# Hybrid decoder layer on one core: the last pair's candidate combination is emitted behind the gate matrices instead of ahead of them

## The chip, the cores and the metric

The kernel runs on one core of one Trainium2 chip. The metric is the device time of one execution in microseconds; the median of three runs of the kernel before is 3168.3 us (3166.18 to 3172.95).

## The reference, cut to what matters

One decoder layer over 1024 tokens of width 1024: a token mixer (dilated attention and a convolution module), a product-key expert layer (PEER), a gated embedding, a final norm. The change lies in PEER:

```python
s_half, i_half = lax.top_k(s, PEER_TOPK)            # 16 best of 128 keys, per token, head and half
cand = (s_half[:, :, 0, :, None] + s_half[:, :, 1, None, :])   # all pairs of the two halves
top_s, top_c = lax.top_k(cand, PEER_TOPK)           # 16 best pairs
expert = i1 * N_KEYS + i2                           # which of 16384 experts
gate = jax.nn.softmax(top_s, axis=-1)
h = einsum('td,tkd->tk', xb, expert_u[eb]);  act = gelu(h) * gb
y = einsum('tk,tkd->td', act, expert_v[eb])         # 128 experts per token (8 heads x 16)
```

## The kernel before, in words

The 1024 tokens are eight tiles of 128 (numbers 0 to 7), and they go through the mixer in four pairs. For every pair the program runs attention and convolution, the output projection, then the **search** (`search`, L467: matmuls with the keys, and on VectorE the 16 best keys per head and half) and the **combination** (`combine`, L499 to L576). The combination adds the 50 pairs of keys that can be among the best 16 (`cand`, L510), takes the 16 best (L520 to L524), a softmax over them (`gate`, L527 to L532, with an Exp on ScalarE at L528), and turns positions into two key numbers `i1` and `i2` by comparisons and sums over 128x2048 bf16 tiles (L535 to L575; two widening copies on ScalarE, L556 and L571).

Two kinds of tiles follow different routes:

- Tiles 2 to 5 (`ALL`) are the **dense tiles**. `gate_matrix` (L637 to L687) writes for each of their tokens the full 128 x 128 matrix of gates to HBM: per group of four tokens, two bf16 matmuls subtract the key number from the token's `i1` (`pd`, L659, L660, in one of three PSUM banks), VectorE turns that into `oa` (L668), `o2` is made on VectorE (L674) or, every second group, on ScalarE (L681, L682), four matmuls multiply them (`pG`, L685), ScalarE copies the result into `stage` (L686), and eight groups fill one stage of 2 MB that SP writes to `gate_d` (L687). That is 128 groups in all. `wide_input` (L689) prepares the tiles' input. Then `dense` (L704) goes through all 16384 experts in 32 steps on TensorE: `ph` (L741 to L743), `py` (L772 to L774).
- Tiles 0, 1, 6 and 7 (`FEW`) are the **gathered tiles**. `places` (L580) makes the expert numbers `ex` from `i1` and `i2` (L582). For each of 128 slots POOL fetches one row per token of `expert_u` and later of `expert_v` by an indirect DMA (L596), into six buffers, and VectorE consumes it: L609 (`u`, a dot product) and L625 (`v`, a sum into `gy`). That is 1024 fetches, tile by tile.

The four pairs are (0,1), (2,3), (4,5), (6,7). So the last pair's combination feeds only the gathered tiles 6 and 7, while the gate matrices need the combinations of the pairs (2,3) and (4,5).

The program is written with a tile framework: its scheduler sets each engine's own order of instructions at build time, by dependencies and by the order of emission, and each engine then works through its list in order. The gathers are written last (`gather_all`, L627), so they take the places on VectorE that other work leaves. What is emitted around the change:

```python
stage_search(NG - 1)                  # L885, search of tiles 6 and 7
stage_combine(NG - 1)                 # L886, their combination
for j, i in enumerate(ALL):           # L887
    gate_matrix(gp, j, *wide[i])      # L888, tiles 2 to 5
wide_input(h1, xh, xl)                # L889
gph.close()                           # L890, frees the space of the gate stages
```

Behind the dense steps, each tile goes through `embed` (L780): for the dense tiles 2 to 5 and the gathered tiles 0, 1, 6 and 7, the last of which is tile 7, whose input `gy` is the sum of its last fetches.

Of the kernel before, what the change touches and what calls it, by code (L numbers as in the profile page):

```python
# [26 lines left out]
NG = len(GROUPS)  # L27
# [74 lines left out]
def tile_layer(ctx, tc, t, consts, out):  # L102
# [38 lines left out]
    def rstd(srcs, n, name, junk=None, pool=small):  # L141

        ssq = pool.tile([P, len(srcs)], F32, tag="ssq", name=f"ssq_{name}", bufs=2)
        for j, src in enumerate(srcs):
            sq = junk(f"sqj_{name}_{j}") if junk else mpool.tile([P, D], BF16, tag="t2", name=f"sqj_{name}_{j}", bufs=3)
            S.activation(sq[:, :n], src, AF.Square, accum_out=ssq[:, j : j + 1])  # L146
        return inv_sqrt(ssq, 1.0 / n, name, pool)
# [432 lines left out]
    def places(i, i1, i2):  # L580
        ex = gpool.tile([P, SLOTS], I32, tag="ex", name=f"ex{i}", bufs=NF)
        V.scalar_tensor_tensor(ex, flat(i1), float(NK), flat(i2), ALU.mult, ALU.add)  # L582
        return ex
# [53 lines left out]
    def gate_matrix(gp, j, i1, i2, gate):  # L637

        tr = []
        for what, src in (("i2", i2), ("g", gate)):  # L640
            f = flat(src)
            if what != "g":
                f32 = mpool.tile([P, SLOTS], F32, tag="t2", name=f"gl{what}{j}", bufs=3)
                S.copy(f32, f)
                f = f32
            pt = pps(f"pgt{what}{j}")
            nc.tensor.transpose(pt[:, 0:P], f, ident)
            d = gp.tile([P, P], F32, tag=f"{what}T", name=f"{what}T{j}", bufs=2)
            S.copy(d, pt[:, 0:P])
            tr.append(d)  # L650
        i2T, gT = tr
        i2N = gp.tile([P, P], F32, tag="i2N", name=f"i2N{j}", bufs=2)
        S.activation(i2N, i2T, AF.Copy, scale=-1.0)
        four = [P, 4, NK]

        def less_keys(ix, t0, name):

            pd = lin(name).rearrange("p (t k) -> p t k", k=NK)
            nc.tensor.matmul(pd, flat(ix), ident16[:, t0 : t0 + 4].unsqueeze(2).to_broadcast(four), start=True, stop=False)  # L659
            nc.tensor.matmul(pd, ones16, minus16.to_broadcast([1, 4, NK]), start=False, stop=True)  # L660
            return pd

        for b in range(P // BT):
            stage = gp.tile([P, NK, BT], F32, tag="stage", name=f"stage{j}_{b}", bufs=2)
            for o in range(0, BT, 4):
                t0 = b * BT + o
                oa = gp.tile(four, F32, tag="oa", name=f"oa{j}_{t0}", bufs=2)
                V.scalar_tensor_tensor(  # L668
                    oa, less_keys(i1, t0, f"pd1_{j}_{t0}"), 0.0, gT[:, t0 : t0 + 4].unsqueeze(2).to_broadcast(four),
                    ALU.is_equal, ALU.mult,  # L670
                )
                o2 = gp.tile(four, F32, tag="o2", name=f"o2_{j}_{t0}", bufs=3)
                if o % 8 == 0:
                    V.tensor_tensor(  # L674
                        o2, i2T[:, t0 : t0 + 4].unsqueeze(2).to_broadcast(four),
                        iota.unsqueeze(1).to_broadcast(four), ALU.is_equal,
                    )
                else:

                    for e in range(4):  # L680
                        S.activation(o2[:, e, :], iota, AF.Abs, bias=i2N[:, t0 + e : t0 + e + 1])  # L681
                    S.activation(o2, o2, AF.Relu, bias=1.0, scale=-1.0)  # L682
                pg = sps(f"pG{j}_{t0}")
                for e in range(4):
                    nc.tensor.matmul(pg[:, rows(e)], o2[:, e, :], oa[:, e, :], start=True, stop=True)  # L685
                S.copy(stage[:, :, o : o + 4], pg.rearrange("p (t i) -> p i t", i=NK))  # L686
            nc.sync.dma_start(gd[j, :, :, b], stage.rearrange("p (q c) t -> p q (c t)", c=GROUP))  # L687

    def wide_input(h1, xh, xl):  # L689

        for q, h in enumerate(h1):
            r = rstd([h], D, f"wide{q}")
            xn = mpool.tile([P, D], F32, tag="xn", name=f"xw{q}", bufs=2)
            V.scalar_tensor_tensor(xn, h, r, g_ffn, ALU.mult, ALU.mult)
            for b in range(0, KD, 4):
                pt = pps(f"pt_xw{q}_{b}")
                for i in range(4):
                    nc.tensor.transpose(pt[:, rows(i)], xn[:, rows(b + i)], ident)
                hi, lo = (a[:, b : b + 4, rows(q)] for a in (xh, xl))
                pt = pt.rearrange("p (m c) -> p m c", c=P)  # L700
                S.copy(hi, pt)
                V.tensor_tensor(lo, pt, hi.bitcast(F32), ALU.subtract)
# [142 lines left out]
    def stage_search(g):  # L845
        st[g] = search(g, st[g])

    def stage_combine(g):
        vals, idxs = st[g]
        for j, i in enumerate(GROUPS[g]):  # L850
            if i in FEW:
                i1, i2, gate = combine(i, vals[j], idxs[j], gpool, NF)
                fetched[i] = (places(i, i1, i2), gate)
            else:
                wide[i] = combine(i, vals[j], idxs[j], mpool, ND)
# [27 lines left out]
    minus16 = gp.tile([1, 1, NK], BF16, name="minus16")  # L883
    V.tensor_scalar(minus16[:, 0, :], iota[0:1, :], -1.0, None, ALU.mult)
    stage_search(NG - 1)  # L885
    stage_combine(NG - 1)  # L886
    for j, i in enumerate(ALL):  # L887
        gate_matrix(gp, j, *wide[i])  # L888
    wide_input(h1, xh, xl)  # L889
    gph.close()  # L890
    den_in, du = scope(ctx, name="dupool", side="right")
# [90 lines left out]
```

## Time and profile before

| | us |
|---|---|
| median of three runs | 3168.3 |
| the profiled execution | 3160.1 |
| its span | 3158.3 |
| search of the last pair ends on VectorE | 1163.3 |
| first and last `pG` matmul of the gate matrices | 1192.1, 1408.7 |
| first dense matmul | 1437.9 |
| first matmul of the embeddings (L796) | 2963.1 |

| engine | busy, share of the span |
|---|---|
| TensorE (PE) | 87% |
| VectorE (DVE) | 79% |
| GpSimd (POOL) | 47% |
| ScalarE (ACT) | 36% |

Times of instructions are microseconds from the start of the span. A row of a timeline gives start, duration, engine, line, operation, what it writes and reads, and in square brackets the idle time of the engine before it with what ended that. The granted clock of TensorE is a share: 1.00 is 2.4 GHz, 0.50 is 1.2 GHz.

### The profile page before, as it was taken

The numbers are of one execution on the slowest core, as the hardware profiler recorded it, in microseconds if no ns is written. First come the engines' busy times: TensorE is split into PE (matmuls) and PEld (weight loads), VectorE is DVE, ScalarE is ACT, GpSimd is POOL, SyncE is SP. The second block draws the span as 40 slices with busy tenths as digits, with TensorE's granted clock in tenths as the row PEclk, the third lists the DMA queues.
The fourth block names the chain that finished last, engine by engine and source line by source line (L and its number), as shares of the span: only waits on it lengthen the run. The fifth ranks groups of instructions, "written<-read, shape, count | busy, mean of one in ns | idle before, by whom it ended". The sixth has DMA issues, their size and how long they took to land. (4 is left out here: it accounts for less than half of the span.)

```text
span 3158.3 us, 36012 instructions
## 1 busy us (share of the span) xinstructions
PE 2740.0 (87%) x11711; PEld 2003.6 (63%) x11711; DVE 2504.5 (79%) x5164; ACT 1132.6 (36%) x2082; POOL 1487.7 (47%) x1220
## 2 busy tenths in 40 slices
PE   6588959968995768987999999999999999999996
PEld 3465625853673455656777777777777777777643
DVE  1528777998898799886988888888988888988851
ACT  3523443264245228872232222232232232232342
POOL 0401675465445521224555556556655556555620
PEclk9798978988997888998999999999999999999998
DMA  5154859847953855999999999999999999999840
GB/s 164 54 179 148 311 200 347 293 147 260 338 188 129 321 202 169 284 274 345 340 333 343 322 339 344 356 340 351 332 323 344 353 329 349 348 324 335 323 159 23
DMA packets 304526, 865.75 MB, mean 274 GB/s; under 512 B 26778, under 2 KB 93746, under 8 KB 304338
## 3 DMA queue, kind: packets, MB, share of 16 engines
q0 software_dynamic: 147456, 536.94, 46.7%
q1 hardware_dynamic: 153616, 323.16, 29.7%
q10 hardware_dynamic: 3266, 3.36, 0.3%
q8 instruction: 92, 1.51, 0.2%
q14 instruction: 96, 0.79, 0.1%
HBM read 819.83 MB, written 43.52 MB: 273 GB/s over the span
## 5 line engine op out<-in xcount | busy, mean ns | idle before, releaser
L596 POOL DMA_INDIRECT u<-in_expert_u_dram,ex x512 | 654.4, 1278 | 830.1 <-DVE hk L609 568.0
L596 POOL DMA_INDIRECT v<-in_expert_v_dram,ex x512 | 682.3, 1333 | 513.0 <-DVE gy L625 380.6
L625 DVE SCALAR_TENSOR_TENSOR gy<-v,ga,gy 128x1024 f32<-128x1024 f32 x512 | 657.7, 1285 | 41.6 <-DMA v<-in_expert_v_dram,ex 32.6
L609 DVE CUSTOM_DVE_ANT_0 u<-u,gxn 128x1024 f32<-128x1024 f32 x512 | 613.1, 1226 | 52.3 <-DMA u<-in_expert_u_dram,ex 49.7
L741 PE MATMUL ph<-xh,uh 128*128 128x512 f32 x1024 | 407.1, 398 | 44.0 <-ACT uh L717 43.9
L743 PE MATMUL ph<-xh,ul 128*128 128x512 f32 x1024 | 409.4, 400 | 25.6 <-DVE ul L719 25.4
L742 PE MATMUL ph<-xl,uh 128*128 128x512 f32 x1024 | 405.1, 396 | 0.0
L759 ACT CAST vh<-v 128x1024 fp32r<-128x1024 f32 x128 | 131.5, 1051 | 749.0 <-PE kept_y L774 484.8
L741 PEld LDWEIGHTS ph<-xh,uh 128*128 128x128 f32 x1024 | 195.8, 191 | 91.8 <-ACT uh L717 51.9
L743 PEld LDWEIGHTS ph<-xh,ul 128*128 128x128 f32 x1024 | 195.6, 191 | 82.4 <-DVE ul L719 42.1
L350 POOL TENSOR_TENSOR side<-side,tap 128x256 f32<-128x256 f32 x192 | 150.8, 787 | 194.6 <-ACT tap L349 133.6
L761 DVE TENSOR_TENSOR vl<-v,vh 128x1024 fp32r<-128x1024 f32 x128 | 154.0, 1223 | 108.5 <-ACT vh L759 108.0
L772 PE MATMUL py<-vh,ah 128*128 128x512 f32 x512 | 204.0, 399 | 37.3 <-ACT ah L751 37.2
L270 PE MATMUL pq<-x2T,w_pq 128*128 128x256 f32 x1024 | 231.2, 384 | 5.6 <-DMA w_pq<-in_peer_wq_dram 3.9
L742 PEld LDWEIGHTS ph<-xl,uh 128*128 128x128 f32 x1024 | 195.9, 191 | 42.0
L270 PEld LDWEIGHTS pq<-x2T,w_pq 128*128 128x128 f32 x1024 | 194.6, 193 | 34.3 <-DMA w_pq<-in_peer_wq_dram 3.5
L773 PE MATMUL py<-vl,ah 128*128 128x512 f32 x512 | 200.4, 394 | 0.0
L774 PE MATMUL kept_y<-vh,al 128*128 128x512 f32 x512 | 199.7, 390 | 0.0
L772 PE MATMUL kept_y<-vh,ah 128*128 128x512 f32 x512 | 199.7, 390 | 0.0
L773 PE MATMUL kept_y<-vl,ah 128*128 128x512 f32 x512 | 199.5, 390 | 0.0
L774 PE MATMUL py<-vh,al 128*128 128x512 f32 x512 | 198.3, 395 | 0.3 <-DVE al L753 0.3
L717 ACT CAST uh<-u 128x1024 fp32r<-128x1024 f32 x128 | 134.1, 1048 | 113.7 <-DMA u<-in_uT_dram 80.2
(264 smaller groups left out, 4691.4 us busy)
## 6 DMA issues: line engine op xcount, KB each, us to landing
u<-in_uT_dram SPq DMA_DIRECT2D x128, 512.0 KB
v<-in_expert_v_dram SPq DMA_DIRECT2D x128, 512.0 KB
w_pq<-in_peer_wq_dram SPq DMA_DIRECT2D x64, 512.0 KB
gate_d<-stage SPq DMA_DIRECT2D x16, 2048.0 KB
gt<-gate_d SPq DMA_DIRECT2D x64, 512.0 KB
w_o<-in_w_out_dram SPq DMA_DIRECT2D x32, 512.0 KB
w_k<-in_w_qkv_dram SPq DMA_DIRECT2D x16, 512.0 KB
w_q<-in_w_qkv_dram SPq DMA_DIRECT2D x16, 512.0 KB
```

What stands on the lines that cost most here:

```text
L270: nc.tensor.matmul(a, w[:, k, :], xT[:, k, :], start=k == 0, stop=k == KD - 1)
L350: G.tensor_tensor(side, side, m, ALU.add)
L596: d = G.indirect_dma_start(out=e, out_offset=None, in_=table, in_offset=bass.IndirectOffsetOnAxis(ap=index, axis=0))
L609: uses(V.tensor_tensor_reduce(out=e, in0=e, in1=xn, scale=1.0, scalar=0.0, op0=ALU.mult, op1=ALU.add, accum_out=hk[:, k : k + 1]))
L625: uses(V.scalar_tensor_tensor(y, e, act[:, k : k + 1], y, ALU.mult, ALU.add))
L741: nc.tensor.matmul(ph, hi, xh[:, k, :], start=k == 0, stop=False)
L742: nc.tensor.matmul(ph, hi, xl[:, k, :], start=False, stop=False)
L743: nc.tensor.matmul(ph, lo, xh[:, k, :], start=False, stop=k == KD - 1)
L761: V.tensor_tensor(b, v, a.bitcast(F32), ALU.subtract)
L772: nc.tensor.matmul(py, ah[e][:, rows(j)], vh[e][:, half(f)], start=first, stop=False)
L773: nc.tensor.matmul(py, ah[e][:, rows(j)], vl[e][:, half(f)], start=False, stop=False)
L774: nc.tensor.matmul(py, al[e][:, rows(j)], vh[e][:, half(f)], start=False, stop=last_e)
```

## The change

The call that combines the pair (6,7) is emitted behind the four gate matrices.

```diff
@@ -883,9 +883,9 @@
     minus16 = gp.tile([1, 1, NK], BF16, name="minus16")
     V.tensor_scalar(minus16[:, 0, :], iota[0:1, :], -1.0, None, ALU.mult)
     stage_search(NG - 1)
-    stage_combine(NG - 1)
     for j, i in enumerate(ALL):
         gate_matrix(gp, j, *wide[i])
+    stage_combine(NG - 1)
     wide_input(h1, xh, xl)
     gph.close()
     den_in, du = scope(ctx, name="dupool", side="right")
```

Since the scheduler decides, three places of the engines' orders show what moves. On VectorE, behind the last operation of the search, first as it was before (`cand6` and `top6` are tile 6's candidates and its best ones, `oa0_0` and `o2_0_0` the first group of the first gate matrix):

```order
L496 MAX_INDEX idxs3_1_6393<-vals3_1_6392,sc3_3_1_6796 128x8 x2
L510 TENSOR_TENSOR cand6_6818<-vals3_0_6390 128x8x16
...
L535 CAST ix6_6875<-idxs3_0_6391 128x256
L520 MAX top6_6826<-cand6_6818 128x8 x2
...
L510 TENSOR_TENSOR cand7_6911<-vals3_1_6392 128x8x8
L668 SCALAR_TENSOR_TENSOR oa0_0_7017<-pd1_0_0_7018,gT0_7012 128x512
L530 TENSOR_REDUCE gs6_6871<-gate6_6868 128x8
L520 MAX top7_6919<-cand7_6911 128x8
```

and as it is with the change:

```order
L496 MAX_INDEX idxs3_1_6393<-vals3_1_6392,sc3_3_1_6796 128x8 x2
L668 SCALAR_TENSOR_TENSOR oa0_0_6831<-pd1_0_0_6832,gT0_6826 128x512
L674 TENSOR_TENSOR o2_0_0_6836<-i2T0_6822,cst_85 128x512
L668 SCALAR_TENSOR_TENSOR oa0_4_6844<-pd1_0_4_6845,gT0_6826 128x512
L674 TENSOR_TENSOR o2_0_8_6866<-i2T0_6822,cst_85 128x512
L510 TENSOR_TENSOR cand6_8818<-vals3_0_6390 128x8x16
...
L535 CAST ix6_8875<-idxs3_0_6391 128x256
L668 SCALAR_TENSOR_TENSOR oa0_8_6861<-pd1_0_8_6862,gT0_6826 128x512
L520 MAX top6_8826<-cand6_8818 128x8 x2
```

The first two `oa` and `o2` now stand ahead of the combination, and the rest of the combination is spread between the groups: `ex` of tile 6 (L582) stands behind 47 of the 128 `oa` (behind 1 before), that of tile 7 behind 85 (behind 12 before). Between the first and the last `oa` stood 40 `u` products of the gathers (L609); now 25 stand there, and 10 instead of 11 behind the last one, ahead of the dense steps. On SP a few transfers of the gathered tiles (L606, L926, L928) move by some places among the dense loads; POOL's order is unchanged.

On ScalarE, behind the squares of `wide_input`, before:

```order
L146 ACTIVATE sqj_wide3_0_9074,ssq_wide3_9073<-h1_5_4627 128x1024
L528 ACT_TABLE_LOAD
L528 ACTIVATE gate6_6868<-gate6_6868 128x128
L556 COPY ge6_6879<-p166_6877 128x2048
L571 COPY eq6_6900<-p166_6877 128x2048
L528 ACTIVATE gate7_6961<-gate7_6961 128x128
L556 COPY ge7_6972<-p167_6970 128x2048
L681 ACTIVATE o2_0_4_7035<-cst_85,i2N0_7014 128x128 x4
```

and with the change, there and, behind the dots, at the group of tokens 60 of the first matrix:

```order
L146 ACTIVATE sqj_wide3_0_9074,ssq_wide3_9073<-h1_5_4627 128x1024
L681 ACTIVATE o2_0_4_6849<-cst_85,i2N0_6828 128x128 x4
L682 ACTIVATE o2_0_4_6849<-o2_0_4_6849 128x512
...
L681 ACTIVATE o2_0_60_7061<-cst_85,i2N0_6828 128x128
L528 ACT_TABLE_LOAD
L528 ACTIVATE gate6_8868<-gate6_8868 128x128
L686 COPY stage0_1_6952<-pG0_56_7050 128x128x4
```

The Exp of tile 6 and that of tile 7 each stand between groups now, each with a table load ahead of it and, behind it, one for the next square root (L151): four loads among the gate matrices, where there were two, one of them ahead of the first group.

On VectorE, in the embeddings behind the dense steps, before (`v7_125` to `v7_127` are tile 7's last fetched rows, `sg1_4` the gate of the embedding of tile 4):

```order
L813 TENSOR_TENSOR sg1_4_18621<-sg1_4_18621,plp4_1_18623 128x512
L625 SCALAR_TENSOR_TENSOR gy7_21633<-v7_125_22010,ga7_21630,gy7_21633 128x1024
L814 TENSOR_TENSOR h1_4_4625<-h1_4_4625,sg1_4_18621 128x512
L625 SCALAR_TENSOR_TENSOR gy7_21633<-v7_126_22013,ga7_21630,gy7_21633 128x1024
L625 SCALAR_TENSOR_TENSOR gy7_21633<-v7_127_22016,ga7_21630,gy7_21633 128x1024
L153 RECIPROCAL r_fin4_18633<-sd_fin4_18631 128x1
```

and with the change, there and at the end of the gathers:

```order
L813 TENSOR_TENSOR sg1_4_18621<-sg1_4_18621,plp4_1_18623 128x512
L625 SCALAR_TENSOR_TENSOR gy7_21633<-v7_108_21959,ga7_21630,gy7_21633 128x1024
L814 TENSOR_TENSOR h1_4_4625<-h1_4_4625,sg1_4_18621 128x512
...
L813 TENSOR_TENSOR sg0_0_19501<-sg0_0_19501,plp0_0_19503 128x512
...
L625 SCALAR_TENSOR_TENSOR gy7_21633<-v7_127_22016,ga7_21630,gy7_21633 128x1024
L813 TENSOR_TENSOR sg1_0_19517<-sg1_0_19517,plp0_1_19519 128x512
```

At the same operation of tile 4 the gathers are 17 rows behind; the last one stands directly ahead of the second half of tile 0's embedding (`sg1_0`). Behind the last addition of the dense steps (L778) there are 56 `v` sums, where there were 40; in the dense steps themselves the number is the same, 20 or 21 a step. On TensorE the order behind the dense steps is unchanged.

## Rows read from the trace of the kernel before

**Rows 1.** Busy time of each engine by stretch; then clock, DMA share, GB/s.
```profile
core 0: us, PE busy (x) PEld busy (x) DVE busy (x) ACT busy (x) POOL busy (x), PEclk, DMA share, GB/s
1163.30:1192.00 28.70, 1.12 (x2) 0.10 (x1) 28.70 (x179) 8.16 (x10) 0.00 (x0) 0.50 0.00 1
...
1199.10:1409.00 209.90, 204.24 (x1282) 139.28 (x1280) 184.60 (x303) 183.36 (x454) 40.45 (x41) 1.00 0.83 252
1163.30:1409.00 245.70, 212.10 (x1309) 144.79 (x1308) 219.29 (x490) 197.08 (x476) 40.45 (x41) 0.92 0.71 216
1500.00:2900.00 1400.00, 1325.93 (x5672) 1067.92 (x5671) 1228.85 (x1609) 370.18 (x478) 825.30 (x602) 0.99 0.94 339
2963.00:3060.00 97.00, 96.89 (x279) 48.24 (x280) 68.88 (x69) 37.44 (x81) 44.38 (x37) 0.97 0.68 248
```

**Rows 2.** Timeline of TensorE: start, duration, instruction, idle time before it.
```profile
1172.86 0.58 PE L659 MATMUL pd<-ident,i 128*128 128x512 bf16 x1 [13.17 <-DVE oa L668]
...
1192.11 2.07 PE L685 MATMUL pG<-oa,o 128*128 128x128 f32 x8 [18.13 <-DVE o L674]
...
1195.39 3.78 PE L685 MATMUL pG<-oa,o 128*128 128x128 f32 x16 [0.24 <-ACT o L682]
...
1407.80 1.16 PE L685 MATMUL pG<-oa,o 128*128 128x128 f32 x8 [1.35 <-ACT o L682]
```

**Rows 3.** Timeline of VectorE, from the end of the search to `ex` of tile 7.
```profile
1163.31 0.96 DVE L510 TENSOR_TENSOR cand<-vals 128x128 f32<-128x128 f32 x7
...
1172.13 0.68 DVE L668 SCALAR_TENSOR_TENSOR oa<-pd,gT 128x512 f32<-128x512 f32 x1
...
1191.37 0.68 DVE L674 TENSOR_TENSOR o<-i2T,cst 128x512 f32<-128x512 f32 x1
...
1215.26 0.28 DVE L582 SCALAR_TENSOR_TENSOR ex<-i,i 128x128 int32<-128x128 bf16 x1
```

**Rows 4.** VectorE's groups from 1163.2 to 1217: busy, mean ns, idle before.
```profile
L668 DVE SCALAR_TENSOR_TENSOR oa<-pd,gT 128x512 f32<-128x512 f32 x13 | 8.8, 681 | 1.8 <-PE pG L685 1.8
L674 DVE TENSOR_TENSOR o<-i2T,cst 128x512 f32<-128x512 f32 x7 | 4.8, 684 | 0.0
```

**Rows 5.** VectorE's group of `u` products from 1300 to 1400.
```profile
L609 DVE CUSTOM_DVE_ANT_0 u<-u,gxn 128x1024 f32<-128x1024 f32 x19 | 23.0, 1216 | 0.0
```

**Rows 6.** Timeline of ScalarE: last square, a widening copy, a table load between two groups.
```profile
1164.80 0.19 ACT L146 ACTIVATION_READ_ACCUMULATOR sqj_wide<-h 128x1 f32 x1
...
1182.59 1.90 ACT L571 COPY eq<-p 128x2048 bf16<-128x2048 bf16 x1 [9.49 <-DVE p L569]
...
1211.56 0.58 ACT L686 COPY stage<-pG 128x512 f32<-128x512 f32 x1
1212.16 1.28 ACT L151 ACT_TABLE_LOAD   x1
1213.45 0.30 ACT L151 ACTIVATE sd_wide<-ssq_wide,eps 128x1 f32<-128x1 f32 x1
```

**Rows 7.** Waits of SP's queue from 1380 to 1450: total, times, longest.
```profile
SPq L715 <- DMA gate_d<-stage: 22.5, 1, 22.5
```

**Rows 8.** Timeline of VectorE behind the dense steps.
```profile
2948.68 1.28 DVE L625 SCALAR_TENSOR_TENSOR gy<-v,ga,gy 128x1024 f32<-128x1024 f32 x1 [1.47 <-DMA v<-in_expert_v_dram,ex]
...
2965.36 1.28 DVE L625 SCALAR_TENSOR_TENSOR gy<-v,ga,gy 128x1024 f32<-128x1024 f32 x1 [1.27 <-DMA v<-in_expert_v_dram,ex]
...
3030.23 2.60 DVE L625 SCALAR_TENSOR_TENSOR gy<-v,ga,gy 128x1024 f32<-128x1024 f32 x2
...
3059.96 0.69 DVE L813 TENSOR_TENSOR sg<-sg,plp 128x512 f32<-128x512 f32 x1 [7.17 <-PE plp L812]
...
3126.46 0.16 DVE L153 RECIPROCAL r_ple<-sd_ple 128x1 f32<-128x1 f32 x1 [1.00 <-ACT sd_ple L151]
```

**Rows 9.** Timeline of POOL: two fetches of tile 7, first and last of 33.
```profile
2973.73 1.01 POOL L596 DMA_INDIRECT v<-in_expert_v_dram,ex  x1 [0.30 <-issue]
...
3024.72 1.01 POOL L596 DMA_INDIRECT v<-in_expert_v_dram,ex  x1 [0.30 <-issue]
```

## The prediction

> **What bounds the kernel now.** I read the stretches first. In the dense steps TensorE is busy 1325.9 of 1400 us at a granted clock of 0.99, with VectorE at 1228.9 [rows 1]: TensorE sets the pace, and VectorE has little room beside it. The 97 us behind them are full too, 96.9 us of TensorE [rows 1]. So whatever lets the dense steps start earlier moves all that follows, unless something else holds the end. The stretch to look at is the one just ahead, the gate matrices. There, from 1163.3 to 1192.0, TensorE is busy 1.1 of 28.7 us and its clock is at 0.50, the lower of its two levels, while VectorE is busy all of the time [rows 1]. The timeline of TensorE names the wait: 13.17 us for `oa`, then 18.13 us for `o2`, both VectorE's, until the first `pG` at 1192.11 [rows 2]. And the timeline of VectorE says what it did instead: the candidates of tile 6 from 1163.31, the first `oa` only at 1172.13, the first `o2` at 1191.37, the last operation of the combination at 1215.26 [rows 3]. From 1199.1 to 1409.0 the picture is the other one: TensorE is busy 204.2 of 209.9 us at full clock, VectorE 184.6, ScalarE 183.4 [rows 1]. That part is TensorE's.
>
> **The price of the combination.** From 1163.31 to the end of `ex` at 1215.54 are 52.2 us. Of these VectorE was idle 1.8, and 13 `oa` took 8.8 and 7 `o2` took 4.8 us [rows 3, 4]. The remainder, 52.2 - 15.4 = 36.8 us, is the combination of two tiles, with a few small things. No gate matrix reads it. The edit removes none of it; it lets the groups of gate matrices go ahead, and the order of VectorE confirms that: two `oa` and two `o2` now stand directly behind the search.
>
> **The start, a gain.** The search ends at 1163.31, where the combination starts today. One `oa` and one `o2` behind it (0.68 us each [rows 3, 4]), so at 1164.7, the first `pG` can start, and not at 1192.11: 27.4 us earlier. ScalarE is ready for the second group soon after: its last square ends at 1164.99 [rows 6], and the Exp that stood next is gone from there. Beyond that, the first groups today run at the lower clock: 8 `pG` rows take 2.07 us there, 16 take 3.78 [rows 2], and a `pd` takes 0.58. TensorE would wait from 1159.7 to 1164.7, 5 us, and not until 1192.1 [rows 2]. If it keeps its clock it saves, over the first three groups and their `pd`, about half of the time from 1192.1 to 1199.1, up to 3 us; if not, nothing. I take 1.6, in the middle. Together 29 us.
>
> **What it costs in the gate matrices.** The combination is now work between the groups, and each engine works in order. Does it fit? VectorE was busy 219.3 us from 1163.3 to 1409, with everything in it; between the first and the last `oa` now stand 25 products of the gathers where 40 stood, and 15 x 1.22 = 18.3 us go [rows 1, 5]. That leaves 201 us. ScalarE has 197.1 us there and gets two more table loads of 1.28 us: about 200 [rows 1, 6]. TensorE needs the 209.9 us from the third group on. So TensorE remains the longest, but the other two are at 95%, and there are only three banks of `pd` to take up unevenness. The lower bound of the new stalls is 0, since by the sums all fits; the upper is the whole 36.8 us, if every operation of the combination stood in TensorE's way. I take 6, near the lower end, because the totals leave 9 us of room and the order spreads the combination over 85 groups: the two table loads (2.6 us) and of each of the four widening copies of 1.90 us [rows 6], which stand between copies out of PSUM, nearly half.
>
> On such a load the row shows 1.28 us, from 1212.16, with the copy ahead of it ended at 1212.14 and the next activation at 1213.45 [rows 6]: nothing around it. The Trainium skill speaks more strongly against the change here (ScalarE: Activation LUTs, section What ACT_TABLE_LOAD costs): about 1283 ns for the load plus about 1380 ns of drain, 2.66 us for a switch to another set. By that the two loads would be 5.3 us and my sum some 3 us worse; the trace has the load but not the drain, and the trace decides.
>
> **From the gate matrices to the dense steps.** The first dense load waits 22.5 us for the last stage to be written [rows 7], because it takes that space. Nothing of this changes: 10 products of the gathers stand there, where 11 stood. It moves with the stages. On SP and POOL only the place of a few loads of the gathered tiles among the dense loads shifts by some rows; if one came too late, it would cost one fetch, under 3 us. The combination issues no DMA.
>
> **The dense steps** keep 20 or 21 gathered rows a step in both orders, so they keep their pace and move as a block: 0.
>
> **The end, a small loss.** Sixteen products that no longer fit among the gate matrices push the gathers back: 56 sums, not 40, stand behind the dense steps. The last two now start at 3030.23 and end at 3032.8 [rows 8]. At POOL's rate there, 33 fetches in 50.99 us from first to last [rows 9], 1.59 us each, sixteen more end 25.5 us later relative to the dense steps, at what is 3058.3 in today's count. The next operation behind them on VectorE is `sg` of tile 0, ready at 3059.96 because TensorE delivers then [rows 8]. That is just in time, with other work in between, so I put 2 us, between 0 and 6. Tile 7's own embedding needs `gy` only before 3126.46 [rows 8] and has ample room. The three embeddings at the end are serial and move as they are.
>
> **Sum.** -29 + 6 + 2 = **-21 us**. On the profiled execution, 3160.1 us (its span of 3158.3 and 1.8 around it), that is 3139.1. The median of the three runs stands 8.2 us above that execution; I take this distance along: 3168.3 - 21 = **3147.3 us**, faster by 0.7%.
>
> **Rivals.**
>
> *The gathers hold the end.* If the sixteen deferred fetches cost what they cost just behind the dense steps, where VectorE waited for their DMA, seven in 16.7 us from 2948.68 to 2965.36, so 2.8 us from one to the next [rows 8], they need 45 us where 27.2 are free (3059.96 less 3032.8). Then tile 0's embedding and the three behind it come 18 us late: -29 + 6 + 18 = -5, 3163 us. For it: VectorE works in order, and the embeddings stand behind the fetches. Against it: those waits fell where the embeddings' weights were loaded, and from 2973.73 POOL kept to 1.59. Chance 0.10, half of it within 0.2%.
>
> *VectorE becomes the bound of the gate matrices, and the kernel is slower.* Place: the 85 groups between which the combination lies. Mechanism: TensorE has three banks ahead; whenever a long bf16 operation or one that waits for ScalarE stands ahead of an `oa`, TensorE runs dry. If all 36.8 us come out as waits, the sum is -29 + 37 + 2 = +10: 3178 us. It turns the sign once TensorE loses over 27 us, three quarters of the combination. For it: two engines at 95% in a fixed order. Against it: VectorE's sum is 201 against 210, and its products of the gathers, already in such places, left TensorE busy 204.2 of 209.9 us [rows 1]. Chance 0.06.
>
> *Between the two*, half of the combination shows as waits: -29 + 18 + 3 = -8, 3160 us. Chance 0.08, three quarters faster.
>
> *The change doesn't do what it says*, because the scheduler decides. The orders exclude most of that; what is left is that the combination's spread hides something that I don't see, with no change in time, 3168 us. Chance 0.03.
>
> **How the numbers follow.** The forecast has 0.73; its own range, with stalls of 1 to 13 us, the clock's 0 to 3 and the end's 0 to 6, is 3139 (-31 + 1 + 0, rounded) to 3160 (-27 + 13 + 6). To hold 8 in 10 the range takes in the rival of the end: 3139 to 3163. A measurement of this kernel can tell about 0.2%, 6.3 us, from no change. Faster by more: 0.73 + 0.05 + 0.06 = 0.84. Within it: 0.05 + 0.02 + 0.03 = 0.10. Slower: 0.06.
>
> **What would show it.** The first `pG` starts within 2 us of the end of the search, and the granted clock stays near 1.00 there. The last `pG` comes 20 to 26 us earlier, and the same shift stands at the first dense matmul and at the first of the embeddings. Between the groups VectorE is nearly full, with little of TensorE idle. The last `v` sum ends at about the same absolute time as now, some 25 us later relative to the dense steps. I would be wrong if TensorE showed repeated waits for `oa` between the groups, adding up to more than 15 us, or if TensorE waited behind the embeddings of tiles 5 and 0.

## The result, and the profile after

The changed kernel takes 3133.5 us (median of 4 runs, 3130.95 to 3141.12); the kernel before, timed beside it, takes 3167.5 us. The ratio is 0.9904, with a 95% interval of 0.9877 to 0.9931. It is faster, as forecast, but by more: 3133.5 lies 13.8 us below the forecast of 3147.3 and below the range, which began at 3139. The profiled execution of after took 3130.95 us with a span of 3129.1, 29.2 us less than the span before.

TensorE's timeline shows where they come from. A row gives start, duration, instruction, and in brackets the idle time before it.

```profile
1162.76 0.33 PE L647 MATMUL pgti<-cst,gli 128*128 128x128 f32 x1 [0.36 <-ACT gT L649]
1167.95 0.58 PE L659 MATMUL pd<-ident,i 128*128 128x512 bf16 x1 [4.86 <-DVE oa L668]
1168.55 4.20 PE L685 MATMUL pG<-oa,o 128*128 128x128 f32 x24
1172.68 0.39 PE L660 MATMUL pd<-minus,ones 1*128 1x512 bf16 x1
```

The waits of 13.17 and 18.13 us of before [rows 2] are now one of 4.86, and three groups of `pG` (24 rows) are through at 1172.75. On VectorE the first `oa` follows the last row of the search at once, and the combination (L510 and on) begins behind the second `o`:

```profile
1167.03 0.28 DVE L496 FIND_INDEX8 idxs<-vals,sc 128x8 uint32<-128x128 f32 x1
1167.23 0.67 DVE L668 SCALAR_TENSOR_TENSOR oa<-pd,gT 128x512 f32<-128x512 f32 x1
1167.82 0.68 DVE L674 TENSOR_TENSOR o<-i2T,cst 128x512 f32<-128x512 f32 x1
1168.41 0.68 DVE L668 SCALAR_TENSOR_TENSOR oa<-pd,gT 128x512 f32<-128x512 f32 x1
1169.02 0.68 DVE L674 TENSOR_TENSOR o<-i2T,cst 128x512 f32<-128x512 f32 x1
1169.62 0.97 DVE L510 TENSOR_TENSOR cand<-vals 128x128 f32<-128x128 f32 x7
```

The same stretches as in [rows 1], busy time of PE, PEld, VectorE, ScalarE and POOL, then the granted clock:

```profile
1167.20:1172.75 5.55, 4.79 (x26) 4.08 (x25) 5.55 (x24) 5.04 (x14) 0.00 (x0) 0.64 0.00 0
1172.75:1383.20 210.45, 203.07 (x1284) 140.27 (x1284) 193.71 (x436) 192.58 (x463) 23.99 (x25) 1.00 0.72 211
1167.20:1383.20 216.00, 207.85 (x1309) 144.36 (x1308) 199.26 (x458) 197.63 (x476) 23.99 (x25) 0.99 0.70 206
1500.00:2900.00 1400.00, 1332.31 (x5694) 1075.77 (x5693) 1228.64 (x1609) 372.36 (x478) 829.31 (x604) 0.99 0.93 339
2930.00:3030.00 100.00, 95.66 (x279) 47.52 (x280) 90.68 (x87) 38.02 (x82) 64.08 (x55) 0.98 0.93 339
```

The whole combination now lies between the groups, and behind the third group VectorE is busy 193.71 of 210.45 us where it was 184.60 of 209.90; TensorE's time for these groups is the same within 0.7 us. The dense steps look as before. Behind them the deferred sums fill VectorE: 90.68 of 100 us against 68.88 of 97.

TensorE's waits from 1150 to 1440 (total, times, longest):

```profile
PE ph L741 <- DMA gt<-gate_d: 29.0, 1, 29.0
PE pd L659 <- DVE oa L668: 6.3, 5, 4.9
PE pG L685 <- ACT o L682: 3.9, 7, 1.2
PE pG L685 <- DVE oa L668: 1.0, 1, 1.0
PE pG L685 <- ACT stage L686: 0.8, 1, 0.8
```

All waits for `oa` but the first come to 2.4 us. The 29 us ahead of the first dense matmul stand as they did; the row for SP's wait is this one, where before had 22.5 [rows 7]:

```profile
SPq L715 <- DMA gate_d<-stage: 22.7, 1, 22.7
```

To set executions side by side I take six marks, as the first and last starts of a line's instructions give them; for after (ns min/median/max, then first and last start):

```profile
L496 DVE FIND_INDEX8 idxs<-vals,sc x128: 274/284/292, 218.1 to 1167.0; 128x8 uint32<-128x128 f32 x128
L685 PE MATMUL pG<-oa,o x1024: 272/275/583, 1168.5 to 1382.9; 128*128 128x128 f32 x171
L741 PE MATMUL ph<-xh,uh x1024: 387/389/793, 1412.2 to 2903.4; 128*128 128x512 f32 x171
L796 PE MATMUL pt_ple<-dg,h x112: 273/276/583, 2927.8 to 3072.6; 128*128 128x128 f32 x112
L625 DVE SCALAR_TENSOR_TENSOR gy<-v,ga,gy x512: 1244/1284/1767, 661.9 to 3028.0; 128x1024 f32<-128x1024 f32 x171
```

The table holds the same marks of all profiled executions, in us. "Search" is the start of its last row (L496); first `pG`, last `pG` and first `ph` count from there; "dense" runs from the first `ph` to the first matmul of an embedding (L796); the last `v` sum (L625) and the end of the span count from that one. In before, that matmul starts at 2957.4; the 2963.1 of the table ahead of the prediction is its second group of rows, behind a wait of 4.63 us.

| kernel | search | first `pG` | last `pG` | first `ph` | dense | last `v` | end | span |
|---|---|---|---|---|---|---|---|---|
| before | 1163.1 | +29.0 | +245.6 | +274.8 | 1519.5 | +74.1 | +200.9 | 3158.3 |
| before_again | 1161.4 | +29.0 | +248.8 | +277.8 | 1518.6 | +74.3 | +201.2 | 3159.0 |
| after | 1167.0 | +1.5 | +215.9 | +245.2 | 1515.6 | +100.2 | +201.3 | 3129.1 |
| after_again | 1175.8 | +1.5 | +217.5 | +246.9 | 1521.4 | +100.3 | +201.4 | 3145.5 |
| no_combine | 1172.4 | +1.5 | +216.1 | +247.2 | 1518.5 | +66.7 | +201.9 | 3140.0 |
| twice | 1168.6 | +1.5 | +220.5 | +245.7 | 1509.9 | +147.8 | +208.5 | 3132.7 |
| four_times | 1166.0 | +1.6 | +219.0 | +293.4 | 1517.4 | +165.5 | +208.2 | 3185.0 |
| half | 1153.9 | +9.5 | +229.5 | +260.6 | 1523.5 | +92.8 | +201.6 | 3139.6 |
| behind_wide | 1162.6 | +1.5 | +216.0 | +246.8 | 1517.0 | +106.4 | +201.2 | 3127.6 |
| one_gate_first | 1228.0 | -143.9 | +164.4 | +194.6 | 1514.5 | +106.9 | +203.3 | 3140.4 |
| gates_first | 1393.8 | -303.2 | -88.2 | +53.6 | 1522.5 | +74.2 | +203.1 | 3173.0 |

From before to after: the search ends 3.9 us later and the dense steps are 3.9 us shorter, neither of which the change touches; last `pG` -29.7; from there to the first `ph` +0.1 (0.0 unrounded); end +0.4. Together -29.2.

### The profile page after: what moved, and what is told of

It reads as the page before. It is cut to its first block, busy times and chain, and to the rows that moved or that the text cites. A ratio compares the mean times of both kernels' runs of the same rounds, so it can differ in the third digit from the quotient of the medians.

```text
span 3129.1 us, 36005 instructions
## 1 busy us (share of the span) xinstructions
PE 2734.5 (87%) x11711; PEld 2003.1 (64%) x11711; DVE 2503.7 (80%) x5164; ACT 1133.9 (36%) x2084; POOL 1495.5 (48%) x1220
## 5 line engine op out<-in xcount | busy, mean ns | idle before, releaser
L596 POOL DMA_INDIRECT u<-in_expert_u_dram,ex x512 | 675.9, 1320 | 822.3 <-DVE hk L609 547.1
L596 POOL DMA_INDIRECT v<-in_expert_v_dram,ex x512 | 671.5, 1312 | 510.7 <-DVE gy L625 376.9
L625 DVE SCALAR_TENSOR_TENSOR gy<-v,ga,gy 128x1024 f32<-128x1024 f32 x512 | 657.8, 1285 | 41.0 <-DMA v<-in_expert_v_dram,ex 31.9
L609 DVE CUSTOM_DVE_ANT_0 u<-u,gxn 128x1024 f32<-128x1024 f32 x512 | 613.7, 1226 | 54.5 <-DMA u<-in_expert_u_dram,ex 53.4
L350 POOL TENSOR_TENSOR side<-side,tap 128x256 f32<-128x256 f32 x192 | 147.8, 772 | 193.8 <-ACT tap L349 132.4
```

What stands on the lines that cost most here:

```text
L350: G.tensor_tensor(side, side, m, ALU.add)
L596: d = G.indirect_dma_start(out=e, out_offset=None, in_=table, in_offset=bass.IndirectOffsetOnAxis(ap=index, axis=0))
L609: uses(V.tensor_tensor_reduce(out=e, in0=e, in1=xn, scale=1.0, scalar=0.0, op0=ALU.mult, op1=ALU.add, accum_out=hk[:, k : k + 1]))
L625: uses(V.scalar_tensor_tensor(y, e, act[:, k : k + 1], y, ALU.mult, ALU.add))
```

## The experiments

**The two kernels again**, unchanged, to see how far two executions of one kernel lie apart (no edit).

> The kernel before, unchanged, once more, to see how far its stages move from one execution to the next. Theory A (the gain is the wait of TensorE ahead of the gate matrices, 27.4 us, and some 3 us of slow clock behind it; what the profile shows besides is spread): the time is that of before within 0.2%; the end of the search moves by some 4 us between executions (1163.3 here, 1167.2 in the changed kernel), and so does the length of the dense steps, from the first ph at 1437.9 to the first matmul of the embeddings at 2957.4, 1519.5 us, against 1515.5 in the changed kernel. Theory B (the change also shortened the dense steps): the dense steps take 1519.5 us within 1 us again.

> The changed kernel, once more, timed in five rounds. Theory A: 29 to 31 us faster than before (ratio 0.990 to 0.991), gate matrices from the end of the search to the last pG 215 to 217 us. Theory B: 33 to 35 us faster (0.989), with dense steps of 1515.5 us within 1 us again, 4 less than before. My prediction's sum (21 us, ratio 0.9934) would need 6 us of stalls in the gate matrices, so 222 us there.

The kernel before came to 3163.7 us, ratio 1.0005 (0.9982 to 1.0028) to its other runs; the change to 3144.2 us, 0.9928 (0.9899 to 0.9956). The change's second trace has the same first `pG`, 1.5 us behind the search, and the same gate matrices within 1.6 us. Its search ends 8.8 us later than in the first trace and its dense steps take 1521.4 us. So the idea that the change shortens the dense steps (1515.6 against 1519.5) has no support: these two stretches vary by that much with nothing changed. The gate matrices of before vary too, 216.6 us in the first trace and 219.8 in the second, where TensorE's mean granted clock over them is 0.98 and 0.97. Differences of 3 us between two single traces of this stretch mean little, therefore, unless the clocks are alike.

**no_combine** leaves the last pair's combination out; tiles 6 and 7 fetch by the numbers and gates of tiles 0 and 1.

```
-    stage_combine(NG - 1)
+    fetched[6], fetched[7] = fetched[0], fetched[1]
```

> The combination of the pair (6,7) is left out altogether; tiles 6 and 7 fetch with the expert numbers and gates of tiles 0 and 1. Left out: 36.8 us of VectorE, 8 us of ScalarE, two table loads. Theory A (all of the combination lies hidden in the changed kernel): the same time as the changed kernel within 2 us, and the gate matrices take 209 to 211 us from the third group on, as with the combination (211.3). The prediction's theory (some 6 us of it stand in TensorE's way): 5 to 7 us faster than the changed kernel.

3139.0 us, ratio 0.9924 (0.9900 to 0.9948). Without the combination the gate matrices take 214.6 us from first to last `pG`; with the change they take 214.4 and 216.0. Taking the combination out altogether wins nothing more that the times show. The comparison is not clean, though. First no_combine, then after, from the first `pG` to the end of the last:

```profile
1173.93:1388.81 214.88, 210.38 (x1308) 145.55 (x1308) 184.64 (x299) 185.67 (x463) 43.55 (x45) 0.98 0.84 254
1168.55:1383.20 214.65, 207.27 (x1308) 144.35 (x1308) 197.91 (x455) 196.31 (x473) 23.99 (x25) 0.99 0.71 207
```

VectorE is only 13 us less busy, not 36.8, because products of the gathers move into the free places (56.89 us of them, 31.87 with the change). And TensorE's clock was lower by a hundredth, which is worth about 2 us of 215 (an estimate from the two rows). So a price of 2 or 3 us for the combination is not excluded; the 5 to 7 us expected from the prediction's theory did not show.

**twice** computes the combination a second time behind the gate matrices; what it gives is not read.

```
     stage_combine(NG - 1)
+    for j in range(2):
+        combine(16 + j, st[NG - 1][0][j], st[NG - 1][1][j], mpool, ND)
```

> The combination of the pair (6,7) is computed a second time behind the first, and nobody reads the second result. 36.8 us more of VectorE, 8 of ScalarE and two more table loads in the gate matrices, and 21 fewer products of the gathers there (4 where 25 stood), so VectorE has about 200 + 37 - 26 = 211 us and ScalarE 208 beside TensorE's 210: no room is left. Theory A (nothing shows as long as the sums fit): the gate matrices grow only by a few us, 3 to 10, and 22 more v sums stand behind the dense steps (79 for 57), which at 1.5 us each is 33 us more than the changed kernel has, where its own last sum is just in time; so the end is held by the gathers, 25 to 35 us later there, and the time is about that of before, 3160 to 3175. If VectorE's stalls set in well before the sums are full, the gate matrices grow by 20 us and more as well, and the time is 3185 or more.

3141.8 us, ratio 0.9933 (0.9913 to 0.9953): the time of the change. The gate matrices grew by a few us, as expected, but the time of 3160 to 3175, with the end held by the gathers, missed. VectorE's stretch shows why the work still fits:

```profile
1168.60:1389.00 220.40, 208.91 (x1292) 145.53 (x1292) 206.63 (x598) 203.56 (x480) 3.75 (x4) 0.98 0.54 153
```

Twice the combination, yet VectorE is only at 206.63 us, since 4 products of the gathers are left among the gate matrices where the change has 25: the order pushes them out behind, 21 of 1.22 us, 25.6 us. The gate matrices are 3 to 5 us longer, not 37, and 1.1 of it stands in the first three groups, which took 5.29 us at the lower clock where the change's trace has 4.20. In the order, 79 `v` sums now stand behind the dense steps (57 with the change, counted in the same way), the last one 47.6 us later than with the change, and the end moves by 7 us only.

**half** puts tile 6's part of the combination ahead of the gate matrices again and leaves tile 7's behind.

```
-    def stage_combine(g):
+    def stage_combine(g, only=(0, 1)):
...
+            if j not in only:
+                continue
...
     stage_search(NG - 1)
+    stage_combine(NG - 1, (0,))
     for j, i in enumerate(ALL):
         gate_matrix(gp, j, *wide[i])
-    stage_combine(NG - 1)
+    stage_combine(NG - 1, (1,))
```

> Of the last pair's combination, tile 6's part stands ahead of the gate matrices again, tile 7's stays behind them; 29 products of the gathers lie among the gate matrices (25 with the whole change, 40 before). Theory A (the gain is the wait for the combination, which TensorE no longer spends idle): half of the wait comes back. The first pG starts 13 to 17 us behind the search, where it was 29 before and 1.5 with the change, the clock falls to its lower level in that wait, and the time is 13 to 19 us above the change's. Theory C (the gain comes from the products of the gathers that left the stretch, which relieved VectorE): 11 of the 15 are gone, so nearly all of the gain stays; at most 8 us above the change's.

3149.1 us, ratio 0.9945 (0.9924 to 0.9966), 16.0 us above behind_wide, which ran on the same chip. The first `pG` comes 9.5 us behind the search, sooner than the 13 to 17 expected, because the first `oa` is taken in among tile 6's operations:

```profile
1162.75 0.59 PE L659 MATMUL pd<-ident,i 128*128 128x512 bf16 x1 [12.36 <-DVE oa L668]
1163.35 2.08 PE L685 MATMUL pG<-oa,o 128*128 128x128 f32 x8
...
1168.06 3.58 PE L685 MATMUL pG<-oa,o 128*128 128x128 f32 x16
```

```profile
1153.90:1171.64 17.74, 8.23 (x30) 5.84 (x29) 17.74 (x101) 9.81 (x19) 0.00 (x0) 0.50 0.00 1
```

But the clock is then at its lower level, 0.50, and stays there over the first three groups, which end at 1171.64, 17.7 us behind the search; with the change that is 5.7, before 36.1. The last `pG` is 12 to 14 us later than with the change. Half of the combination ahead costs about half of the gain, although 11 of the 15 products of the gathers have left the stretch: it is the wait, not the relief of VectorE, that the change wins by.

**behind_wide** emits the combination behind the widening of the dense inputs.

```
-    stage_combine(NG - 1)
     wide_input(h1, xh, xl)
+    stage_combine(NG - 1)
```

> The combination is emitted one place later still, behind the widening of the inputs of the dense steps; 21 products of the gathers lie among the gate matrices, 60 sums behind the dense steps. Theory A: the wait ahead of the gate matrices is gone already, so nothing is left to win: the time of the change within 4 us, first pG 1.5 us behind the search, gate matrices 214 to 217 us long. Theory P (the combination between the groups still costs TensorE stalls of about 6 us, as predicted): the combination lies later among the groups, nothing changes by more than 3 us either. Theory G (deferred gathers hold the end): four more fetches behind the dense steps, 6 us later, which would show as an end more than 201.5 us behind the first embedding.

3133.1 us, ratio 0.9900 (0.9877 to 0.9924), the change's time; the gate matrices take 214.5 us, and four more deferred sums move the last `v` sum by 6.2 us and the end by none. Nothing is left to win at this place.

**one_gate_first** and **gates_first** emit one or all four gate matrices ahead of the last pair's search, where TensorE has gaps; the combination stays behind them all.

```
+    gate_matrix(gp, 0, *wide[ALL[0]])
     stage_search(NG - 1)
-    for j, i in enumerate(ALL):
+    for j, i in enumerate(ALL[1:], 1):
         gate_matrix(gp, j, *wide[i])
     stage_combine(NG - 1)
```

```
-    stage_search(NG - 1)
     for j, i in enumerate(ALL):
         gate_matrix(gp, j, *wide[i])
+    stage_search(NG - 1)
     stage_combine(NG - 1)
```

> The first gate matrix is emitted ahead of the last pair's search, the other three and the combination behind it. In the change's trace TensorE is busy 94 of 150 us from 950 to 1100, and VectorE 123. Theory I (TensorE's idle time there can take a gate matrix, some 52 us): up to 25 us faster than the change, as much as VectorE has idle there. Theory V (VectorE and the loads of the search set the pace there, and VectorE's part of a gate matrix, about 20 us or more, delays the search): the search ends 15 to 40 us later, the three other matrices take 160 us, and the time is within 10 us of the change's or above it.

> All four gate matrices are emitted ahead of the last pair's search, the combination stays behind them all. Theory I: the search hides in the gate matrices, so that both end earlier than the two in a row: 20 to 50 us faster than the change, bounded by VectorE's sum, 429 of 484 us from 900 to 1384 in the change's trace. Theory V: VectorE is the bound of the mixture, the search ends last, and the combination stands behind it with nothing of TensorE's to cover it: 10 to 40 us slower than the change, with TensorE's wait at the end of the search.

With one matrix ahead: 3142.2 us, ratio 0.9910 (0.9883 to 0.9936), no different from the change. The search ends 52 to 61 us later than in the two traces of the change, more than the 15 to 40 expected; the three other matrices take 164.4 us behind it, and the first `ph` starts at 1422.6 us, where the change has 1412.2 and 1422.7. With all four: 3166.1 us, 0.9993 (0.9973 to 1.0013); the whole gain is gone, as theory V had it. TensorE's waits from 1390 to 1450 and the busy times of the stretch behind its search name the cause:

```profile
PE pt_xw L698 <- DVE xw L694: 31.5, 1, 31.5
PE pt_xw L698 <- DVE xl L702: 18.8, 7, 4.9
```

```profile
1394.00:1448.00 54.00, 9.53 (x34) 6.26 (x35) 53.96 (x221) 15.74 (x18) 5.83 (x5) 0.50 0.13 39
```

VectorE is busy 53.96 of 54 us, TensorE 9.53 at the lower clock: the combination stands again with nothing of TensorE's beside it, and this time the widening of the dense inputs waits for it.

**four_times** computes the combination three times more, to find where it stops being free.

```
+    for j in (0, 1, 2, 3, 4, 5):
+        combine(16 + j, st[NG - 1][0][j % 2], st[NG - 1][1][j % 2], mpool, ND)
```

> The last pair's combination is computed three times more behind the gate matrices, the results unread: VectorE gets another 73 us or so beside what the doubled combination gave it. 2 products of the gathers are left among the gate matrices, none up to the first dense column, and 90 sums stand behind the dense steps (79 with the doubled one, 57 with the change). Theory B (VectorE becomes the bound once its sum passes TensorE's; the doubled combination stayed below because 21 products of the gathers made room, and now nothing is left that can make room): gate matrices and transition together 40 to 75 us longer than the 244 us of the doubled one. Theory F (the combination is background that runs into whatever gap there is, also into the dense steps): less than 20 us longer. The end, whichever holds: 11 more sums behind the dense steps at 2.1 us each, so the end 208.5 + 15 to 25 us behind the first embedding.

3195.0 us, ratio 1.0103 (1.0070 to 1.0136): slower than before. The gate matrices are no longer for it (217.5 us), but behind them VectorE has what is left over:

```profile
1387.00:1460.00 73.00, 6.17 (x22) 4.11 (x23) 72.92 (x321) 19.11 (x18) 0.00 (x0) 0.50 0.25 79
```

VectorE is full for 72.92 of 73 us and TensorE waits 43.4 and 19.9 us for `xl` and `xw`:

```profile
PE pt_xw L698 <- DVE xl L702: 43.4, 4, 18.6
PE pt_xw L698 <- DVE xw L694: 19.9, 1, 19.9
```

From the search to the first `ph` it is 47.7 us more than with the doubled one, as theory B had it. VectorE as the bound is real, and it is reached between two and four combinations. The end, expected 15 to 25 us later than the doubled kernel's 208.5, is at 208.2 with 11 more sums behind the dense steps.

## Why the prediction was right and wrong

The mechanism held, but for the clock at the start; the size of one term, the stalls in the gate matrices, was off by most, and the range had no room for how executions differ. Of the 13.8 us by which the forecast missed, 8.2 are terms of the sum (-29.2 where it had -21: the stalls 5.3, the end 1.6, the start 1.3), and 5.6 come from the distance between profiled execution and median: 8.2 us for before, taken along unchanged, 2.6 for after.

- **The start, taken at -29.** From the end of the search to the end of the third group it was 36.1 us and is 5.7 (1172.75 - 1167.03), so -30.3 with the marks unrounded. The wait is 27.5 of it: `pG` 1.3 us behind the first `oa`, against 28.8 us from the start of the combination before. The other 2.9 are the three groups themselves, which took 1199.17 - 1192.11 = 7.06 us and take 4.20. The clock is half of that: the `pG` rows took 1.87 (from 1192.11 to 1193.98) and 3.78 us and now take 4.20 together, 1.45 less. The other 1.41 us, 1193.98 to 1195.39, are 0.24 of idle time and two `pd` that stood behind the first group:

```profile
1193.98 0.63 PE L659 MATMUL pd<-ident,i 128*128 128x512 bf16 x1
1194.54 0.60 PE L660 MATMUL pd<-minus,ones 1*128 1x512 bf16 x1
```

With the change no `pd` stands between the three groups. So the clock's 1.6 came out in size, but by luck: it was the middle between a clock that is kept and one that is not, and neither happened. The clock does not stay near 1.00, it is 0.64 over that stretch, and the first `pd` takes 0.58 us again. It is back by 1172.68, where a `pd` takes 0.39.
- **What it costs in the gate matrices, taken at +6.** This is the step that failed. It measured +0.7: from the end of the third group to that of the last 209.79 us before, 210.45 after, both at a granted clock of 1.00. The totals were right (VectorE 201 forecast, 199.26 measured; ScalarE 200 and 197.63), and so was the conclusion that all fits. The mistake was to add a price for unevenness on top, by counting two table loads and half of each widening copy as stalls of TensorE. TensorE's waits for `oa` behind the first come to 2.4 us in the whole stretch, and of no_combine's two rows 2 or 3 us is the most that can be read as the combination's price. On the load, the trace of after repeats what [rows 6] showed, and not the drain of the Trainium skill (ScalarE: Activation LUTs, section What ACT_TABLE_LOAD costs): the operation ahead ends at 1191.15, the next starts with the end of the load.

```profile
1190.75 0.40 ACT L681 ACTIVATE o<-cst,i2N 128x128 f32<-128x128 f32 x1
1191.18 1.28 ACT L528 ACT_TABLE_LOAD   x1
1192.47 0.31 ACT L528 ACTIVATE gate<-gate 128x128 f32<-128x128 f32 x1
```

- **The transition, 0.** 0.0; the wait for the last stage is 22.7 us. Right.
- **The dense steps, 0.** Right within what executions show (1515.6 and 1521.4 after, 1519.5 and 1518.6 before).
- **The end, taken at +2.** The last `v` sum comes 26.1 us later relative to the dense steps (25.5 forecast), which is 1.63 us for each of 16; the end moves by 0.4. The rows behind the dense steps show the fit: the last four sums stand ahead of `sg` of the second half of tile 0's embedding, and VectorE still waits 0.94 us for TensorE there:

```profile
3024.08 5.24 DVE L625 SCALAR_TENSOR_TENSOR gy<-v,ga,gy 128x1024 f32<-128x1024 f32 x4
3030.26 0.69 DVE L813 TENSOR_TENSOR sg<-sg,plp 128x512 f32<-128x512 f32 x1 [0.94 <-PE plp L812]
```

The one new wait of TensorE there is this:

```profile
2984.89 2.05 PE L796 MATMUL pt_ple<-dg,h 128*128 128x128 f32 x16 [1.33 <-ACT dg L791]
```

- **The rivals.** The gathers holding the end fell: 1.63 us per fetch, not 2.8, and in twice and four_times 22 and 33 more sums move the end by 7 us each. VectorE as the bound fell for this change, but is the mechanism that makes four_times slower; the point at which it decides lies higher than priced, because the gathers' products give way first. Half of the combination as waits fell by the same 0.7 us.
- **The signs.** The last `pG` came 25.8 us earlier in the span (1408.7 to 1382.9), inside the 20 to 26 named, but only because the search ended 3.9 us later in this execution; from the search it is 29.7.
- **The range.** With the four terms as measured (unrounded -29.3) and the 8.2 us it would have been 3168.3 - 29.3 = 3139.0, on its lower edge. It had bounds for each term and none for the executions: the runs of before reach from 3148.3 to 3181.6, and the median of the change itself came to 3133.5 once and to 3144.2 in its repetition. By runs alone the gain is 14 to 39 us (the ends of both intervals); by the marks from the end of the search to the end of the span, 1995.2 and 1997.6 us before, 1962.1 and 1969.7 after, it is 30.5 between the means.

## What to carry to other kernels

Emit work that only a late consumer reads behind the work that feeds the bounding engine, and price the move by two sums: the wait it removes, and whether each engine's total still fits under the bounding one's in the stretch that takes it in. In this kernel, where the totals fitted and other background work could give way, the unevenness cost next to nothing; where the totals did not fit (four_times), or no covering work was left behind it (gates_first), the price came back. And give the range the spread of whole executions as well as that of the terms.

## What was not expected of the hardware

- The stretches ahead of the change and the dense steps vary by many us between executions: the search ends between 1153.9 and 1175.8 us in the nine executions of kernels whose edits all lie behind that mark and in which TensorE, VectorE and POOL go through the same instructions in the same order up to it, and the dense steps take 1509.9 to 1523.5 us. Where this comes from the runs don't settle; TensorE's waits for `w_o` from DRAM, up to 1150 us, came to 13.9 us in before and 21.2 in after_again.
- With the change TensorE does five single transposes of 0.33 us, then waits 4.86 us, and the next `pd` runs at the lower clock (0.58 us); behind the three groups a `pd` takes 0.39 us again. In half, behind the wait of 12.36 us, the `pd` rows stay at 0.58 to 0.61 us until the third group. The forecast's sign had the clock near 1.00 behind the shorter wait.
- With the doubled combination the transition from the last `pG` to the first `ph` took 25.2 us and not 29 to 31. POOL is busy there 8.75 of 25 us, against 12.28 of 28 in the change, so fewer fetches ran beside the last stage's write. That they are the cause was not tried by itself.

```profile
1389.00:1414.00 25.00, 3.68 (x20) 2.40 (x18) 13.89 (x24) 4.46 (x7) 8.75 (x7) 0.59 0.87 302
```

```profile
1384.00:1412.00 28.00, 0.00 (x0) 0.00 (x0) 10.06 (x18) 0.95 (x1) 12.28 (x10) 0.54 0.95 346
```
